# Score matmul of the small key halves over 128 rows instead of 64, and a new order of the next pair's projections

## The chip, the cores and the metric

The kernel runs on one core of a Trainium2 chip. The metric is the device time of one execution in microseconds (us). The core has a matrix engine (PE, with its weight loads shown as PEld), a vector engine (DVE), a scalar engine (ACT), a GpSimd engine (POOL), and a queue engine (SP) that issues nearly all DMA transfers here. Each engine works through its own instructions in order.

## The reference

A decoder trunk of two layers over 1024 tokens of 1024 features, in f32. Each layer has twelve mixer heads of 64 features and four memory heads, one output projection, and a gated feed-forward block with a short convolution. Layer 0 mixes with a forgetting bias, layer 1 with rotary embedding and a fixed table of dilated windows.

```python
sc = einsum('bhqd,bhkd->bhqk', qi, k) * scale      # layer 0
sc = sc + ci[..., :, None] - c[..., None, :]
sc = where(kpos <= qpos, sc, NEG); p = softmax(sc)
out = einsum('bhqk,bhkd->bhqd', p, v)
...
h = h + merge_heads(concat([mix, mem_out])) @ w_out
h = h + conv_ffn(rmsnorm(h, norm_ffn), w_up, conv_w, conv_b, w_down)
```

## The kernel before, in words

Every f32 operand is split into a large half (hi) and a small rest (lo), and a product is made of three PE passes: hi·hi, hi·lo, lo·hi (`mm3g`, L162 to L164). Activations stand transposed, features on the 128 partitions; tokens are cut into two halves of 512.

The attention phase of a layer handles the twelve mixer heads as six pairs. A pair's queries and keys are projected by `proj_q` and `proj_k`, each in two halves of 512 tokens; a half takes 24 matmuls of 512 columns. For each head, the 128 rows of a query tile (qa, qb) hold the head's 64 features of hi and the 64 of lo. The key tile (ka, kb) holds the keys' hi twice, the second copy made by a DMA from SP (`move`, L95), so that one matmul over 128 rows gives (q hi + q lo)·(k hi). The keys' lo of both heads share one tile kl, 64 rows each.

A step is one tile of 128 queries of one head: eight steps i = 0..7 make a head, sixteen a pair, 96 a layer. `scores` (called from `emit_s`) makes the scores of step i against (i+1)*128 keys, in pieces of at most 512 columns: L376 over 128 rows, L377 over 64 rows (q hi · k lo), and in layer 0 for the last piece of a step a mask matmul in bf16 (L379). A layer has 144 pieces (over both layers: 48 each of 128, 256 and 384 columns, and 144 of 512). DVE then adds the bias and takes the extreme (L380), ACT the exponential (L384), DVE the reciprocal and the scaling (L386, L387). Two steps later PE transposes the result (L393) and ACT and DVE split it (L394, L395); one more step later, for two steps at a time, PE multiplies with the values (L692), and `fold` sends the rows to memory.

What PE does between these is other work, dealt out by `Fill`: a list of generators (projections of the next pair, values of the next two pairs by `proj_v`, at the end the output projection `out_part`), each with a cost, a deadline and an earliest step. At each step `Fill.at` sets a rate from the costs and deadlines, and `Fill.go` issues groups of three matmuls by it. PE's order is that in which the code is written; for the other engines a scheduler sets it. Key and query tiles come from a pool of ten (`qk`).

`out_part` reads the other pairs' attention output back through SP (`oraw`, L253); ACT and POOL split it (L254, L255).

Of the kernel before, what the change touches and what calls it, by code (L numbers as in the profile page):

```python
# [29 lines left out]
def trunk(ctx, tc, a, out):  # L30
# [90 lines left out]
    def norm_stages(acc, psum, n=4):  # L121
        """acc [P, n*128]: sums of squares per partition -> PSUM [P, n*128], rstd on each partition."""
        st = psum()
        for t in range(n):
            nc.tensor.matmul(st[:, t:t + 1], lhsT=acc[:, t * P:(t + 1) * P], rhs=ones[:, 0:1], start=True, stop=True)
        ms = small("nms")
        nc.vector.tensor_scalar(ms[:, :n], st[:, :n], 1.0 / T, EPS, op0=ALU.mult, op1=ALU.add)
        rs = small("nrs")
        nc.gpsimd.tensor_tensor(rs[:, :n], ms[:, :n], mhalf[:, :n], op=ALU.pow)
        dg = sqt("dg").rearrange("p (n q) -> p n q", n=4)  # L130
        nc.vector.tensor_tensor(dg[:, :n, :], ident.unsqueeze(1).to_broadcast([P, n, P]),  # L131
                                rs[:, :n].unsqueeze(2).to_broadcast([P, n, P]), op=ALU.mult)
        yield None
        rb = psum()
        nc.tensor.matmul(rb[:, :n * P], lhsT=ones, rhs=dg[:, :n, :], start=True, stop=True)  # L135
        yield rb
# [10 lines left out]
    def norm_split(h_k, rb, gi, hi, lo):  # L147
        """hi/lo of h * rstd * gain for each feature tile."""
        for k in range(KD):
            w = h_k(k).shape[-1]  # L150
            xn = sqt("xn")
            nc.vector.scalar_tensor_tensor(xn[:, :w], h_k(k), gains[:, gi, k:k + 1], rb[:, :w],
                                           op0=ALU.mult, op1=ALU.mult)
            nc.scalar.copy(hi(k), xn[:, :w])
            eng = nc.gpsimd if k % 2 else nc.vector
            eng.tensor_tensor(lo(k), xn[:, :w], hi(k).bitcast(F32), op=ALU.subtract)

# [1 line left out]
    def mm3g(ps, whi, wlo, xhi, xlo, nk, cost=0, first=True, last=True):  # L159
        """ps = sum_k w_k^T x_k; yields after each k."""  # L160
        for k in range(nk):
            nc.tensor.matmul(ps, lhsT=whi(k), rhs=xhi(k), start=(first and k == 0), stop=False)  # L162
            nc.tensor.matmul(ps, lhsT=whi(k), rhs=xlo(k), start=False, stop=False)  # L163
            nc.tensor.matmul(ps, lhsT=wlo(k), rhs=xhi(k), start=False, stop=(last and k == nk - 1))  # L164
            yield 3 * cost
# [11 lines left out]
    def put_v(dst, ps):  # L177
        """dst [P, 2, 128] <- even head [hi | lo], odd head [lo | hi]."""
        s = ps.rearrange("p (h d) -> p h d", h=2)
        f = dst.rearrange("p h (s d) -> p (h s) d", s=2)  # L180
        dh = f[:, 0::3, :]
        nc.scalar.copy(dh, s)
        nc.vector.tensor_tensor(f[:, 1:3, :], s, dh.bitcast(F32), op=ALU.subtract)

# [48 lines left out]
    def h_tiles(half):  # L233
        """residual stream, one half of the tokens, transposed: f(n) -> [P, HT]."""
# [11 lines left out]
    def load_o(l, half):  # L246
        """hi/lo of rows of O^T, but for the last pair's."""
# [29 lines left out]
    # ================= attention phase =================  # L277
    def attention_phase(l):
        with tc.manual_schedule(engines={mybir.EngineType.PE}):
# [6 lines left out]
            vts = {}  # L286

            def proj_v(g):
                """values of two pairs: a generator for each half of the tokens."""
# [29 lines left out]
            def proj_fm(hl, half, rope):  # L319
                """128 projected features (two heads) x 512 tokens, in f32."""  # L320
# [15 lines left out]
            def proj_q(wi, half, dst, rope):  # L336
                """queries of two heads: a stack of (hi, lo) for each."""
# [10 lines left out]
            def proj_k(wi, half, dst, rope):  # L348
                """keys of two heads: hi twice for each, lo of both in one."""
                if half == 0:  # L350
                    dst["w" + str(wi)] = load_w(a[f"wq{l}"][wi])
                    dst["k"], dst["kl"] = (qk("ka"), qk("kb")), qk("kl")
                src, eng = yield from proj_fm(dst["w" + str(wi)], half, rope)
                hs = slice(half * HT, half * HT + HT)
                for i, t in enumerate(dst["k"]):
# [3 lines left out]
                    eng.tensor_tensor(dst["kl"][r, hs], src[r, :], t[r, hs].bitcast(F32), op=ALU.subtract)  # L359
# [3 lines left out]
            def proj_qk(p, half):  # L363
                yield from proj_q(2 + 2 * p, half, ops[p], l == 1)
                yield from proj_k(3 + 2 * p, half, ops[p], l == 1)

# [1 line left out]
            def scores(y, m, qst, q2, kst, k2, i, nk, bias, tri):  # L368
                qs = slice(i * P, (i + 1) * P)
                npc = (nk + HT - 1) // HT  # L370
                for pc in range(npc):
# [5 lines left out]
                    nc.tensor.matmul(sw, lhsT=q2[:, qs], rhs=k2[:, c0:c1], start=False, stop=not mask)  # L377
# [19 lines left out]
            def fold(o, odd, c, half):  # L397
                """sum of the products with V's hi and lo halves -> rows of O^T in DRAM."""
# [96 lines left out]
            def forget():  # L495
                """c = cumsum(log_sigmoid(z)) over tokens; -8c goes to c_scr as rows."""
# [29 lines left out]
            class Fill:  # L526
                """pieces of other products, spread over the steps so that each is done by its deadline."""
# [68 lines left out]
            kms = [k.rearrange("p (x h t) -> p x h t", x=2, h=2) for k in (vk[:, T:], qk("km"))]  # L596
# [23 lines left out]
            QK, V, OP = 48 * 216, 96 * 113, 168 * 216  # L620
            v0 = proj_v(0)
            if l == 0:
# [4 lines left out]
                fill.add(proj_qk(0, 0), QK, 0)  # L627
                fill.add(f, 0, 0)
                fill.add(proj_qk(0, 1), QK, 0)
            else:  # L630
                fill.add(proj_qk(0, 0), QK, 0)
                fill.add(proj_qk(0, 1), QK, 0)
# [6 lines left out]
            for p in range(1, NPAIR):  # L639
                g = p // 2  # L640
                v = proj_v(g) if p % 2 == 0 else None
                fill.add(proj_qk(p, 0), QK, 16 * p - (1.5, 2.5)[l], 16 * p - 16, ("a", p))
                fill.add(proj_qk(p, 1), QK, 16 * p + (2.5, 1.5)[l], 16 * p - 16, ("b", p))
                if v:
                    fill.add(v[0], V, 16 * p + 2, 16 * p - 13, ("va", p))
# [7 lines left out]
            def emit_s(s):  # L653
# [12 lines left out]
                rows = slice(64 * hh, 64 * hh + 64)  # L666
                scores(y, m, qst[hh], qst[hh][rows, :], kst[hh], kl[rows, :], i, (i + 1) * P, bias, l == 0)
# [62 lines left out]
    # ================= output projection and FFN =================  # L730
    def ffn_phase(l):
# [130 lines left out]
def _layouts(i):  # L862
# [5 lines left out]
    def fm(w, n):  # L868
        """[.., 1024, n*128] -> [n, 128, 8*128]: for each block of columns, rows on partitions."""
        return w.reshape(KD, P, n, P).transpose(2, 1, 0, 3).reshape(n, P, KD * P)  # L870

    def nat(w):
        """[1024, n] -> [2, 128, 4*n]"""
# [39 lines left out]
    # constants that depend on shapes alone  # L913
# [35 lines left out]
```

## Time and profile before

| | |
|---|---|
| time, median of 3 runs | 2742.74 us (2741.11 to 2742.86) |
| span of the profiled execution | 2742.4 us |
| PE busy | 2633.8 us (96%) |
| DVE busy | 1467.9 us (54%) |
| ACT busy | 1113.3 us (41%) |
| POOL busy | 894.9 us (33%) |

The profiled execution is given by its span; it lies 0.3 us under the median, so nothing of size lies outside the span. Busy is the share of time in which an engine has an instruction under way. Matmuls overlap, so a busy PE can still lose time inside: what counts there is the distance from one matmul's start to the next one's. PEclk is the granted clock: 1.00 is 2.4 GHz, 0.50 is 1.2 GHz.

### The profile page before, as it was taken

What the parts mean: (1) busy time and instruction counts of PE and PEld (TensorE: products, weight loads), DVE (VectorE), ACT (ScalarE), POOL (GpSimd) and SP (SyncE); (2) the same over time, 40 slices, a digit from 0 to 9 for tenths busy, and PEclk for the clock granted to TensorE, in tenths of its full rate; (3) what the DMA queues carried; (4) which work ended last, traced back from release to release, by engine and by line L of the source; (5) the groups of instructions that cost most, each with busy time, mean ns of one, the idle gap of its engine ahead of it and who ended that gap; (6) DMA issues with size and microseconds to landing.
All of it is one profiled execution on the core that took longest, in us unless ns stands there. A gap on an engine that the chain in (4) does not pass through costs nothing. (4 is left out here: it accounts for less than half of the span.)

```text
span 2742.4 us, 34430 instructions
## 1 busy us (share of the span) xinstructions
PE 2633.8 (96%) x12808; PEld 2129.9 (78%) x12808; DVE 1467.9 (54%) x2879; ACT 1113.3 (41%) x2149; POOL 894.9 (33%) x650
## 2 busy tenths in 40 slices
PE   5999999899999999999998999998899999999997
PEld 4877878667888888888777777776678888888886
DVE  6667666556434342434766766665654343434345
ACT  4555454444313131323355666664443122222222
POOL 4201010345323232323452333335543232322332
PEclk8999999999999999999998999999999999999999
DMA  5122112322111111111331111123111111111112
GB/s 166 47 70 61 46 57 70 121 88 66 50 54 47 47 51 50 47 48 59 127 117 37 42 34 39 39 85 124 64 61 46 54 47 46 51 50 47 47 53 93
DMA packets 95055, 174.65 MB, mean 64 GB/s; under 512 B 11932, under 2 KB 14620, under 8 KB 94888
## 3 DMA queue, kind: packets, MB, share of 16 engines
q1 hardware_dynamic: 94024, 171.77, 19.5%
q8 instruction: 101, 1.65, 0.2%
q10 hardware_dynamic: 864, 0.69, 0.1%
q14 instruction: 66, 0.54, 0.1%
HBM read 148.24 MB, written 15.78 MB: 60 GB/s over the span
## 5 line engine op out<-in xcount | busy, mean ns | idle before, releaser
L110 POOL TENSOR_TENSOR wlo<-wraw,whi 128x512 fp32r<-128x512 f32 x450 | 590.2, 1332 | 1483.8 <-ACT whi L109 1335.0
L162 PE MATMUL bk<-xh,whi 128*128 128x512 f32 x2112 | 863.1, 409 | 32.8 <-ACT xh L254 11.9
L163 PE MATMUL bk<-xl,whi 128*128 128x512 f32 x2112 | 832.4, 394 | 4.2 <-POOL xl L255 2.5
L164 PE MATMUL bk<-xh,wlo 128*128 128x512 f32 x2112 | 830.7, 393 | 0.5 <-POOL wlo L110 0.5
L109 ACT CAST whi<-wraw 128x512 fp32r<-128x512 f32 x450 | 268.2, 616 | 684.4 <-PE bk L163 459.2
L162 PEld LDWEIGHTS bk<-xh,whi 128*128 128x128 f32 x2112 | 402.7, 191 | 125.0 <-ACT xh L254 13.1
L164 PEld LDWEIGHTS bk<-xh,wlo 128*128 128x128 f32 x2112 | 401.0, 190 | 86.4 <-POOL wlo L110 1.2
L163 PEld LDWEIGHTS bk<-xl,whi 128*128 128x128 f32 x2112 | 401.9, 190 | 81.5 <-POOL xl L255 6.2
L162 PE MATMUL bk<-gh,whi 128*128 128x512 f32 x704 | 275.4, 391 | 1.2 <-DVE h L259 1.1
L767 DVE SCALAR_TENSOR_TENSOR gate<-bk,cw,gate 128x511 f32<-128x511 f32 (+1 forms) x176 | 131.2, 746 | 271.3 <-ACT gate L765 269.7
L163 PE MATMUL bk<-gl,whi 128*128 128x512 f32 x704 | 274.1, 389 | 0.0
L164 PE MATMUL bk<-gh,wlo 128*128 128x512 f32 x704 | 273.8, 389 | 0.0
L259 DVE TENSOR_TENSOR h<-h,bk 128x512 f32<-128x512 f32 x208 | 141.6, 685 | 233.8 <-PE bk L164 233.8
L384 ACT ACTIVATE y<-y,m 128x128 f32<-128x128 f32 (+1 forms) x192 | 149.2, 777 | 118.8 <-DVE m L380 116.2
L767 DVE SCALAR_TENSOR_TENSOR val<-bk,cw,val 128x511 f32<-128x511 f32 (+1 forms) x176 | 131.1, 745 | 115.2 <-ACT val L765 113.6
L395 DVE TENSOR_TENSOR ptl<-bk,pth 128x512 fp32r<-128x512 f32 (+3 forms) x288 | 152.8, 552 | 73.6 <-ACT pth L394 71.3
L394 ACT CAST pth<-bk 128x512 fp32r<-128x512 f32 (+3 forms) x288 | 130.5, 479 | 101.7 <-PE bk L393 99.3
L162 PEld LDWEIGHTS bk<-gh,whi 128*128 128x128 f32 x704 | 132.2, 188 | 31.1 <-DVE h L259 2.7
L163 PEld LDWEIGHTS bk<-gl,whi 128*128 128x128 f32 x704 | 132.2, 188 | 27.6 <-issue 0.5
L164 PEld LDWEIGHTS bk<-gh,wlo 128*128 128x128 f32 x704 | 132.2, 188 | 27.5
L783 DVE TENSOR_TENSOR gl<-val,gh 128x1024 fp32r<-128x1024 f32 x44 | 53.9, 1226 | 174.8 <-ACT gh L782 174.8
L779 POOL TENSOR_TENSOR val<-val,gate 128x1024 f32<-128x1024 f32 x44 | 105.8, 2404 | 90.1 <-ACT gate L778 90.1
(160 smaller groups left out, 3662.3 us busy)
## 6 DMA issues: line engine op xcount, KB each, us to landing
wraw<-in_wu SPq DMA_DIRECT2D x176, 256.0 KB, 2.8
wraw<-in_wd SPq DMA_DIRECT2D x104, 256.0 KB, 2.8
wraw<-in_wo SPq DMA_DIRECT2D x64, 256.0 KB, 2.8
wraw<-in_wq SPq DMA_DIRECT2D x56, 256.0 KB, 2.8
oscr<-fold SPq DMA_DIRECT2D x56, 128.0 KB, 2.2
oraw<-oscr SPq DMA_DIRECT2D x28, 256.0 KB, 3.9
cb<-cscr SPq DMA_DIRECT2D x12, 512.0 KB, 3.8
wraw<-in_wv SPq DMA_DIRECT2D x20, 256.0 KB, 2.8
```

What stands on the lines that cost most here:

```text
L109: nc.scalar.copy(hi[:, w], raw[:, :n])
L110: nc.gpsimd.tensor_tensor(lo[:, w], raw[:, :n], hi[:, w].bitcast(F32), op=ALU.subtract)
L162: nc.tensor.matmul(ps, lhsT=whi(k), rhs=xhi(k), start=(first and k == 0), stop=False)
L163: nc.tensor.matmul(ps, lhsT=whi(k), rhs=xlo(k), start=False, stop=False)
L164: nc.tensor.matmul(ps, lhsT=wlo(k), rhs=xhi(k), start=False, stop=(last and k == nk - 1))
L259: nc.vector.tensor_tensor(H[half](n), (src or H[half])(n), ps, op=ALU.add)
L384: nc.scalar.activation(y[:, :nk], y[:, :nk], AF.Exp, bias=m[:, npc - 1:npc], scale=-1.0, accum_out=m[:, 2:3])
L394: nc.scalar.copy(ph, tp[:, :nj, :])
L395: nc.vector.tensor_tensor(pl, tp[:, :nj, :], ph.bitcast(F32), op=ALU.subtract)
L767: nc.vector.scalar_tensor_tensor(t[:, o + d:o + HT], ps[:, :HT - d], w(2 - d), t[:, o + d:o + HT], op0=ALU.mult, op1=ALU.add)
L779: nc.gpsimd.tensor_tensor(v, v, g, op=ALU.mult)
L783: nc.vector.tensor_tensor(gl, v, gh.bitcast(F32), op=ALU.subtract)
```

## The change

The lo halves of the keys get a tile for each head (kla, klb), with the lo rows in both halves of the partitions; the second copy is made by a DMA on SP, as for hi. The second score matmul reads the same 128-row query tile as the first and contracts over 128 rows; it adds q lo · k lo. Queries and keys of the next pair become separate entries of the fill list: queries in the first head of the current pair, then the first half of the values, then keys in the second head. A pair now takes six tiles of the pool of ten instead of five; the memory keys' tile km moves to another pool.

```diff
-                    dst["k"], dst["kl"] = (qk("ka"), qk("kb")), qk("kl")
+                    dst["k"], dst["kl"] = (qk("ka"), qk("kb")), (qk("kla"), qk("klb"))
...
                     nc.scalar.copy(t[r, hs], src[r, :])
                     move(t[o, hs], t[r, hs])
-                    eng.tensor_tensor(dst["kl"][r, hs], src[r, :], t[r, hs].bitcast(F32), op=ALU.subtract)
+                    eng.tensor_tensor(u[r, hs], src[r, :], t[r, hs].bitcast(F32), op=ALU.subtract)
+                    move(u[o, hs], u[r, hs])
...
                     nc.tensor.matmul(sw, lhsT=qst[:, qs], rhs=kst[:, c0:c1], start=True, stop=False)
-                    nc.tensor.matmul(sw, lhsT=q2[:, qs], rhs=k2[:, c0:c1], start=False, stop=not mask)
+                    nc.tensor.matmul(sw, lhsT=qst[:, qs], rhs=klt[:, c0:c1], start=False, stop=not mask)
...
-            kms = [k.rearrange("p (x h t) -> p x h t", x=2, h=2) for k in (vk[:, T:], qk("km"))]
+            km = yt("km").bitcast(R32)
+            kms = [k.rearrange("p (x h t) -> p x h t", x=2, h=2) for k in (vk[:, T:], km)]
...
-            QK, V, OP = 48 * 216, 96 * 113, 168 * 216
+            QK, V, OP = 24 * 216, 96 * 113, 168 * 216
...
-                fill.add(proj_qk(p, 0), QK, 16 * p - (1.5, 2.5)[l], 16 * p - 16, ("a", p))
-                fill.add(proj_qk(p, 1), QK, 16 * p + (2.5, 1.5)[l], 16 * p - 16, ("b", p))
+                fill.add(pair_q(p, 0), QK, 16 * p - 12, 16 * p - 16, ("a", p))
+                fill.add(pair_q(p, 1), QK, 16 * p - 8, 16 * p - 16, ("a", p))
                 if v:
-                    fill.add(v[0], V, 16 * p + 2, 16 * p - 13, ("va", p))
+                    fill.add(v[0], V, 16 * p - 6, 16 * p - 13, ("va", p))
+                fill.add(pair_k(p, 0), QK, 16 * p - (1.5, 2.5)[l], 16 * p - 8, ("a", p))
+                fill.add(pair_k(p, 1), QK, 16 * p + (2.5, 1.5)[l], 16 * p - 8, ("b", p))
+                if v:
                     fill.add(v[1], V, 16 * p + 6, 16 * p - 13, ("vb", p))
```

The lines of the changed file stand three further down here (L376, L377, L379 and L393 become L379, L380, L382 and L396).

PE in layer 0, pair 2, second head, between the scores of steps 45 and 46. Before, with one group of three projection matmuls on either side of the transposes:

```order
L162 MATMUL bk<-xh_567,whi 128x512
L163 MATMUL bk<-xl_568,whi 128x512
L164 MATMUL bk<-xh_567,wlo 128x512
L393 MATMUL bk<-ident,y 128x128 x4
L162 MATMUL bk<-xh_567,whi 128x512
L163 MATMUL bk<-xl_568,whi 128x512
L164 MATMUL bk<-xh_567,wlo 128x512
L376 MATMUL bk<-kb,qb 128x512
```

Of the change, the same place, ahead of it the scores of step 45:

```order
L379 MATMUL bk<-kb,qb 128x512
L380 MATMUL bk<-klb,qb 128x512
L379 MATMUL bk<-kb,qb 128x256
L380 MATMUL bk<-klb,qb 128x256
L382 LDWEIGHTS identb
L382 MATMUL bk<-trim,identb 128x128
L396 MATMUL bk<-ident,y 128x128 x4
L162 MATMUL bk<-xh_567,whi 128x512
L163 MATMUL bk<-xl_568,whi 128x512
L164 MATMUL bk<-xh_567,wlo 128x512
```

One group of three has left this step. Over whole heads the projection work, counted in matmuls of 512 columns, goes in layer 0 from 42, 42 to 48, 36 in the two heads of pair 0, from 66, 80 to 86, 71 in those of pair 1, and from 74, 63 to 96, 36 in those of pair 2; in layer 1 the second heads of pairs 0, 2 and 4 go from 66 to 42 each.

SP in layer 1 near the end of the fifth pair, where the last pair's keys and the read-back for the output projection (oraw) follow each other. Before:

```order
L253 DMA oraw<-oscr_0_87 128x512
L95 DMA ka<-ka 64x512
L95 DMA kb<-kb 64x512
L409 DMA oscr_4_91<-fold 64x512
L253 DMA oraw<-oscr_1_88 128x512
L253 DMA oraw<-oscr_2_89 128x512
```

Of the change:

```order
L253 DMA oraw<-oscr_0_87 128x512
L95 DMA ka<-ka 64x512
L95 DMA kla<-kla 64x512
L95 DMA kb<-kb 64x512
L95 DMA klb<-klb 64x512
L412 DMA oscr_4_91<-fold 64x512
L253 DMA oraw<-oscr_1_88 128x512
L253 DMA oraw<-oscr_2_89 128x512
```

Two copies of lo rows stand between the first and the second read-back.

## Rows read from the trace of the kernel before

**Rows 1.** Windows, attention steps of both layers: length, busy by engine, PEclk, DMA, GB/s.

```profile
168.50:493.20 324.70, 324.27 (x1884) 253.41 (x1883) 225.70 (x602) 170.80 (x393) 34.50 (x27) 1.00 0.20 60
1499.00:1840.40 341.40, 337.11 (x1904) 264.65 (x1903) 233.98 (x609) 219.18 (x478) 111.18 (x85) 1.00 0.16 45
```

**Rows 2.** Timeline of PE, layer 1: start, duration, line, operands.

```profile
1547.19 0.40 PE L376 MATMUL bk<-kb,qb 128*128 128x512 f32 x1
1547.51 0.50 PE L377 MATMUL bk<-kl,qb 64*128 64x512 f32 x1
1547.94 0.39 PE L376 MATMUL bk<-kb,qb 128*128 128x256 f32 x1
...
1548.57 0.50 PE L162 MATMUL bk<-xh,whi 128*128 128x512 f32 x1
1548.91 0.39 PE L163 MATMUL bk<-xl,whi 128*128 128x512 f32 x1
1549.14 0.39 PE L164 MATMUL bk<-xh,wlo 128*128 128x512 f32 x1
1549.37 0.60 PE L393 MATMUL bk<-ident,y 128*128 128x128 f32 x4
...
1550.04 0.39 PE L163 MATMUL bk<-xl,whi 128*128 128x512 f32 x1
```

**Rows 3.** Timeline of PE, layer 0: value products, then masked scores.

```profile
334.80 0.29 PE L692 MATMUL bk<-ptl,vt 128*128 128x256 f32 x1
334.92 0.22 PE L692 MATMUL bk<-pth,vt 128*128 128x128 f32 x1
334.98 0.28 PE L692 MATMUL bk<-ptl,vt 128*128 128x128 f32 x1
...
338.43 0.39 PE L376 MATMUL bk<-kb,qb 128*128 128x512 f32 x1
...
339.68 0.23 PE L379 MATMUL bk<-trim,identb 128*128 128x128 bf16 x1
...
340.03 0.40 PE L163 MATMUL bk<-xl,whi 128*128 128x512 f32 x1
```

**Rows 4.** Timeline of PE's weight loads, layer 0.

```profile
330.86 0.19 PEld L376 LDWEIGHTS bk<-kb,qb 128*128 128x128 f32 x1
331.36 0.18 PEld L377 LDWEIGHTS bk<-kl,qb 64*128 64x128 f32 x1 [0.31 <-issue]
```

**Rows 5.** All waits: PEld at L377, total us and times.

```profile
PEld bk L377 <- issue: 63.1, 228, 0.4
```

**Rows 6.** Windows of three heads, columns as in rows 1.

```profile
168.50:190.80 22.30, 22.30 (x108) 15.39 (x107) 18.32 (x51) 12.58 (x30) 2.55 (x2) 1.00 0.17 47
323.40:355.60 32.20, 32.20 (x172) 24.20 (x171) 22.79 (x60) 16.71 (x37) 1.31 (x1) 1.00 0.15 41
1667.60:1700.50 32.90, 32.90 (x167) 24.58 (x166) 22.30 (x56) 23.04 (x48) 10.76 (x9) 1.00 0.12 33
```

**Rows 7.** Groups of DVE instructions in one head: a query half's subtractions.

```profile
L346 DVE TENSOR_TENSOR qa<-bk,qa 64x512 fp32r<-64x512 f32 x2 | 1.4, 684 | 1.2 <-ACT qa L345 1.1
```

**Rows 8.** Waits of PE: total us, times, longest.

```profile
PE bk L162 <- ACT xh L254: 11.9, 3, 5.8
PE bk L376 <- DMA ka<-ka: 2.3, 2, 1.1
```

**Rows 9.** Timeline of POOL, layer 1: the key's lo rows of one head.

```profile
1548.11 1.28 POOL L359 TENSOR_TENSOR kl<-ropeq,ka 64x512 fp32r<-64x512 f32 x1 [1.46 <-ACT ka L357]
```

**Rows 10.** DMA issues: count, KB each, median us to landing.

```profile
ka<-ka SPq DMA_DIRECT2D x24, 128.0 KB, 2.2
```

**Rows 11.** Window where layer 0's last pair begins, columns as in rows 1.

```profile
493.20:520.00 26.80, 19.81 (x97) 14.16 (x95) 12.76 (x32) 14.08 (x30) 12.57 (x10) 0.87 0.58 183
```

**Rows 12.** Timeline of PE in that window, after its longest wait.

```profile
513.10 0.63 PE L164 MATMUL bk<-xh,wlo 128*128 128x512 f32 x1
513.52 0.63 PE L162 MATMUL bk<-xh,whi 128*128 128x512 f32 x1
```

More of the change, by code (lines that the diff above doesn't have):

```diff
@@ L351, in proj_k @@
                     dst["w" + str(wi)] = load_w(a[f"wq{l}"][wi])
-                    dst["k"], dst["kl"] = (qk("ka"), qk("kb")), qk("kl")
+                    dst["k"], dst["kl"] = (qk("ka"), qk("kb")), (qk("kla"), qk("klb"))
                 src, eng = yield from proj_fm(dst["w" + str(wi)], half, rope)
                 hs = slice(half * HT, half * HT + HT)
-                for i, t in enumerate(dst["k"]):
+                for i, (t, u) in enumerate(zip(dst["k"], dst["kl"])):
                     r, o = slice(64 * i, 64 * i + 64), slice(64 - 64 * i, 128 - 64 * i)
@@ L358, in proj_k, with pair_q, pair_k, scores @@
                     move(t[o, hs], t[r, hs])
-                    eng.tensor_tensor(dst["kl"][r, hs], src[r, :], t[r, hs].bitcast(F32), op=ALU.subtract)
+                    eng.tensor_tensor(u[r, hs], src[r, :], t[r, hs].bitcast(F32), op=ALU.subtract)
+                    move(u[o, hs], u[r, hs])
             ops = {p: {} for p in range(NPAIR)}
[L363 to L368, printed above, removed]
+            def pair_q(p, half):
+                return proj_q(2 + 2 * p, half, ops[p], l == 1)
+            def pair_k(p, half):
+                return proj_k(3 + 2 * p, half, ops[p], l == 1)
+            def scores(y, m, qst, kst, klt, i, nk, bias, tri):
                 qs = slice(i * P, (i + 1) * P)
@@ L626, in attention_phase @@
                 fill.add(f, 0, 0)
-                fill.add(proj_qk(0, 0), QK, 0)
+                fill.add(pair_q(0, 0), QK, 0)
+                fill.add(pair_k(0, 0), QK, 0)
                 fill.add(f, 0, 0)
-                fill.add(proj_qk(0, 1), QK, 0)
-            else:
-                fill.add(proj_qk(0, 0), QK, 0)
-                fill.add(proj_qk(0, 1), QK, 0)
+                fill.add(pair_q(0, 1), QK, 0)
+                fill.add(pair_k(0, 1), QK, 0)
+            else:
+                for half in range(2):
+                    fill.add(pair_q(0, half), QK, 0)
+                    fill.add(pair_k(0, half), QK, 0)
                 fill.add(v0[0], V, 0)
@@ L665, in emit_s @@
                 y, m = yt("y"), new_m()
-                rows = slice(64 * hh, 64 * hh + 64)
-                scores(y, m, qst[hh], qst[hh][rows, :], kst[hh], kl[rows, :], i, (i + 1) * P, bias, l == 0)
+                scores(y, m, qst[hh], kst[hh], kl[hh], i, (i + 1) * P, bias, l == 0)
                 st["y", s] = y
```

## The prediction

> **What bounds the kernel now.** I read the windows over the attention steps first. In layer 0 PE is busy for 324.3 of 324.7 us, in layer 1 for 337.1 of 341.4, at a clock of 1.00; DVE comes next with 70% and 69%, ACT with 53% and 64% [rows 1]. So in these 666 us time is what PE's instructions take from start to start. Nothing outside the attention phases is changed, and they are the only place to look.
>
> Then PE's timeline, for those distances. Between ordinary full matmuls of 512 columns it is 0.23 us (L163 to L164) [rows 2]; for 256 columns it is 0.12, for 128 columns 0.06 [rows 3]. The score matmuls don't keep this. In layer 1 a step with a piece of 512 and one of 256 columns runs from 1547.19 (first L376) to 1548.91 (L163, the second projection matmul behind it): 1.72 us [rows 2]. Its matmuls at the ordinary distances would take three times 0.23 (two halves of the 512 piece, and L162) and two times 0.12, 0.93 in all. The excess is 0.79 us for two 64-row matmuls, **0.395 us each**. In layer 0, 512 and 128 columns with a mask run from 338.43 to 340.03 [rows 3], 1.60 us against 0.69 + 0.12 = 0.81: again 0.79, with the mask's matmul inside it. Small and large pieces lose the same, so it isn't the columns; it is the passage to 64 rows and back. The weight loads show the first half of it: L376's load begins at 330.86, L377's only at 331.36, after an idle 0.31 [rows 4], and such an idle stands before 228 of the 288 loads of L377, 63 us in all [rows 5].
>
> **The change part by part.**
>
> *The second matmul over 128 rows.* Its columns stay, so it costs an ordinary distance, and the excess goes. 288 pieces, 144 per layer, 96 of them with a mask (the last piece of each of layer 0's 96 steps). The 192 without: 192 x 0.395 = **75.8 us**. With a mask, the mask matmul had its time hidden in the passage and will need its own. No row shows a bf16 matmul behind a full f32 one. From below it costs 0.06, as any 128 columns [rows 3]; from above, if its change of type cost what the change of rows does, the whole 0.395. I take the nearest row: four transposes of 128 columns, which also differ in kind from their neighbours, take with one projection matmul 1550.04 - 1549.37 = 0.67 us [rows 2], less 0.23, so 0.11 each. That leaves 0.285 x 96 = **27.4 us** (0 to 32.2).
>
> *The new order of the projections.* PE's total of projection work is the same. But second heads of pairs 0, 2 and 4 now hold 36 (layer 0) or 42 (layer 1) projection matmuls, and there DVE, which has the same scores to treat, comes close to PE. Layer 0, the head at 323.40: 32.2 us for 63 projection matmuls [rows 6]; with 36, 27 x 0.23 = 6.2 less, twelve pieces x 0.395 = 4.7 less, eight masks x 0.11 = 0.9 more: PE 22.2 us. DVE had 22.8; 27 projection matmuls are 27/24 of a half, and each half has two subtractions of 0.684 [rows 7], so 1.5 less: 21.3, or 96% of PE's time. Layer 1, the head at 1667.60: 32.9 - 24 x 0.23 - 4.7 = 22.7 for PE; DVE 22.3 - 1.4 = 20.9, 92%. The first head of layer 0 goes from 42 to 48: 22.3 + 1.4 - 4.7 + 0.9 = 19.9, DVE about 18.7, 94%. The highest share of DVE at which PE lost nothing is that head's 18.3/22.3 = 82% [rows 6]; 100% is out of reach with its waits for ACT. I take 88%: the heads then last 24.1 instead of 22.2 (three of them), 23.8 instead of 22.7 (three), 21.3 instead of 19.9: 5.7 + 3.3 + 1.4 = **10 us lost** (0 at 100%, 22 at 82%). The other heads get more projection work, and DVE is no neighbour there.
>
> *The copies of the keys' lo rows.* 48 more DMAs of 128 KB on SP, which land in 2.2 us like ka's [rows 10]. Before, PE waited for that copy twice, 1.1 us each, in layer 1 [rows 8]. The copy of kla can start only after POOL's subtraction, 1.28 us later than ka's [rows 9]. First halves of the keys now end in the fourth step before their use where the next pair is odd, and second halves earlier than before. So some 1.3 us more at three places in layer 1, less the two old waits: **2 us lost** (0 to 8). In layer 0 the subtraction is on DVE and there is no rotation ahead of it; nothing.
>
> *The same copies in front of the read-back.* SP issues in order, and where the last pair begins, the read-back of the attention output stands behind the last key copies. There PE already waits, 11.9 us over both layers, 5.8 the longest [rows 8]; the window has PE busy for 19.8 of 26.8 us and a clock of 0.87 [rows 11], and behind the wait the distance of two full matmuls is 0.42 us, the lower level of 1.2 GHz [rows 12]. kla and klb stand in this queue now and make the loads wait for DVE (layer 0) or two POOL subtractions (layer 1): 1.4 and 2.6 us. And PE arrives earlier by what it saved in the three steps before (3 to 5 pieces, some 1.5 us, and fewer projection matmuls), which turns into wait. **8 us lost** over both layers (3 to 15, the latter if the lower clock lasts longer).
>
> *At nothing:* the pool of ten tiles (six for a pair, two for the next queries; the four key tiles come when the first head has given three back), and km's move. The cover is the second head, 22 us long; without it keys would wait for the last score of the pair.
>
> Sum: 75.8 + 27.4 - 10 - 2 - 8 = 83 us. From the profiled 2742.4, 2659.2; the median lies 0.3 higher: **2659.5 us**.
>
> **The rivals.**
>
> *The loads stay exposed.* The weights of two neighbouring full matmuls use the same rows of the array. If a load could not run under a matmul of the same rows, two loads of 0.19 [rows 4] would remain of each 0.395, 288 x 0.015 = 4 us would be won, the losses above would be hidden under it, and the time would be about 2742. Against it stands the distance of 0.23 at L163 to L164 [rows 2]: a load of 0.19 doesn't fit beside 512 columns unless it overlaps. The Trainium skill ("TensorE: Matmul & The Clock Gate", Part 3, What overlaps and what doesn't) says that loads overlap with matmuls in flight only when the row group differs; the trace disagrees for full matmuls, and shows the opposite at the change of row group. 2 in 100.
>
> *DVE takes over.* If the masks give nothing back (75.8 alone) and the light heads run at a DVE share of 82%: 75.8 - 22 - 2 - 8 = 44, so 2699. For it: 92 to 96% is more than any stretch before has shown. Against: DVE's work can be put off within a head, since scores run two steps ahead. 10 in 100.
>
> *Slower, by late keys.* The lo copy misses its step at each of the ten pair changes, PE waits, and the clock falls behind the wait as it does in rows 12. A clock of 0.87 over 26.8 us [rows 11] is 7 us at half speed, 3.5 lost. With a wait of 8 us: 10 x 11.5 = 115, so 2742.4 - 83 + 115 = 2774. It decides from 8.9 us per pair change on, which is a wait of 5.4. For it: a wait for ka existed. Against: it was 1.1 us, and only in layer 1. 4 in 100.
>
> **How the numbers follow.** The forecast's case, with losses between their bounds, holds 81 in 100; a larger gain than 105 us 3. With all masks at 0.06 and the least losses (3) the time is 75.8 + 32.2 - 3 = 105 lower, 2637; with the masks at nothing and losses of 22, 8 and 15 it is 31 lower, 2711. The range is 2638 to 2697: it leaves out the upper rivals and the tails. A measurement of this kernel can tell about 0.2% (5.5 us) from no change. Faster by more than that: 0.94; within it: 0.02; slower: 0.04.
>
> **What would show it.** L377's successor (L380) without idle before its weight load, and 0.23 between it and its neighbours at 512 columns; the distance behind the mask shows its price. The light heads, 22 to 24 us long, with DVE at 85 to 92% and PE waiting for DVE's or ACT's tiles there. Waits for kla in layer 1 of 1 to 3 us in all, and the wait at L254 longer than 12. Wrong would be: an idle that stays before the second load; a mask that costs 0.3; or waits of several us at pair changes with the clock down.

## The result, and the profile after

The changed kernel takes 2701.49 us (median of 4 runs, 2698.09 to 2704.73); beside it the kernel before took 2742.80. The ratio is 0.985 (95% interval 0.9836 to 0.9864): some 41 us faster, half of the 83 that were forecast, and above the forecast's range. The profiled executions differ by 2742.4 - 2698.3 = 44.1 us. Of the kernels e1_even and e9_best below, one execution each (4225.05 and 3239.57 us) ran for long at the lower clock and is left out.

In the changed kernel the second score matmul stands on L380 and the mask's on L382; DVE's reduction is L383, the scaling L390, the transposes L396, ACT's and DVE's halves of the split L397 and L398, the value products L701. Heads are counted 0 to 11 in each layer; heads 10 and 11 are the last pair.

Windows of the profile after: the first ten heads of layer 0 and of layer 1, then head 5 of layer 0, head 5 of layer 1, and head 10 of layer 0. Columns as in [rows 1].

```profile
166.30:472.00 305.70, 293.51 (x1891) 253.86 (x1890) 223.69 (x603) 171.73 (x394) 35.83 (x28) 0.99 0.25 72
1471.90:1803.30 331.40, 304.24 (x1910) 265.86 (x1909) 225.41 (x610) 220.89 (x480) 112.88 (x87) 0.99 0.18 49
317.60:343.00 25.40, 22.52 (x145) 19.19 (x144) 21.67 (x59) 16.39 (x37) 2.58 (x2) 1.00 0.27 74
1639.90:1668.10 28.20, 23.89 (x144) 19.98 (x142) 21.82 (x58) 21.16 (x45) 10.22 (x8) 1.00 0.14 38
472.00:516.90 44.90, 39.10 (x202) 30.87 (x201) 24.97 (x65) 24.18 (x50) 19.54 (x15) 0.92 0.50 156
```

Against [rows 1], the ten heads fell from 324.7 to 305.7 us and from 341.4 to 331.4. PE's busy time fell by 30.8 and 32.9 us, but PE, which had 0.4 and 4.3 us without work, now has 12.2 and 27.2. Second heads of an even pair, which [rows 6] shows at 32.2 and 32.9 us, last 25.4 and 28.2, where 24.1 and 23.8 were forecast. DVE's share there is 85% and 77%, below the 88% at which the forecast set its limit, and PE waits all the same.

Timeline of PE after, layer 1, a step with two pieces of 512 columns; columns as in [rows 2].

```profile
1528.48 0.40 PE L379 MATMUL bk<-kb,qb 128*128 128x512 f32 x1
1528.72 0.39 PE L380 MATMUL bk<-klb,qb 128*128 128x512 f32 x1
...
1529.41 0.39 PE L162 MATMUL bk<-xh,whi 128*128 128x512 f32 x1
1529.63 0.40 PE L163 MATMUL bk<-xl,whi 128*128 128x512 f32 x1
```

From the first L379 to L163 it takes 1.15 us: five times 0.23, and no excess is left.

Timeline of PE after, layer 0, a masked step with 512 and 128 columns.

```profile
459.56 0.40 PE L379 MATMUL bk<-kb,qb 128*128 128x512 f32 x1
459.80 0.39 PE L380 MATMUL bk<-klb,qb 128*128 128x512 f32 x1
460.02 0.22 PE L379 MATMUL bk<-kb,qb 128*128 128x128 f32 x1
460.08 0.28 PE L380 MATMUL bk<-klb,qb 128*128 128x128 f32 x1
460.20 0.23 PE L382 MATMUL bk<-trim,identb 128*128 128x128 bf16 x1
460.24 0.48 PE L162 MATMUL bk<-xh,whi 128*128 128x512 f32 x1
460.56 0.40 PE L163 MATMUL bk<-xl,whi 128*128 128x512 f32 x1
```

The like step of before took 1.60 us ([rows 3]); this takes 1.00, which is 0.19 above the ordinary distances. The mask's own distance is only 0.04, but the matmul ahead of it goes on for 0.12 where 128 columns take 0.06, and L162 behind it for 0.32 instead of 0.23. Over all masked steps with a projection matmul behind, the medians by shape lie 0.12 to 0.18 above the ordinary distances, most at 0.13; the mask's own columns are in that.

PE's waits after, first ten heads of layer 1: total us, times, longest.

```profile
PE bk L396 <- DVE ptl L398: 18.7, 16, 2.7
PE bk L701 <- DVE ptl L398: 5.2, 10, 1.0
...
PE bk L380 <- DMA kla<-kla: 0.3, 1, 0.3
```

With two small ones left out here (2.7 us) these are 26.9 of the 27.2 us. In the ten heads of layer 0 the first of them comes to 9.9 us in 12 waits, of 11.9 in all. So PE's transposes now stop for a bank which DVE's L398 has not yet read, 28 times; before, this wait came 2 times in the whole program (3.1 us) and not in these windows. The key copies that the prediction feared cost 0.3 us.

What such a wait looks like, in head 9 of layer 0 (444.9 to 472.0). PE:

```profile
447.25 0.95 PE L396 MATMUL bk<-ident,y 128*128 128x128 f32 x7
...
448.97 0.23 PE L382 MATMUL bk<-trim,identb 128*128 128x128 bf16 x1
451.02 1.32 PE L396 MATMUL bk<-ident,y 128*128 128x128 f32 x8 [1.82 <-DVE ptl L398]
...
452.57 0.63 PE L163 MATMUL bk<-xl,whi 128*128 128x512 f32 x1
453.00 0.63 PE L164 MATMUL bk<-xh,wlo 128*128 128x512 f32 x1
```

ACT in the same stretch:

```profile
447.45 0.62 ACT L109 CAST whi<-wraw 128x512 fp32r<-128x512 f32 x1
448.51 0.58 ACT L345 CAST qb<-bk 64x512 fp32r<-64x512 f32 x1 [0.44 <-DVE qa L346]
449.11 0.97 ACT L397 CAST pth<-bk 128x512 fp32r<-128x512 f32 x2
```

DVE:

```profile
447.79 0.69 DVE L346 TENSOR_TENSOR qa<-bk,qa 64x512 fp32r<-64x512 f32 x1
448.50 1.01 DVE L390 TENSOR_SCALAR y<-y,m 128x128 f32<-128x128 f32 x1
449.55 0.69 DVE L346 TENSOR_TENSOR qb<-bk,qb 64x512 fp32r<-64x512 f32 x1
450.27 1.16 DVE L398 TENSOR_TENSOR ptl<-bk,pth 128x512 fp32r<-128x512 f32 x2
```

Seven transposes fill both of the transposes' banks by 448.20. ACT could split them from then on, but a query half that was just projected stands ahead in its queue: qb's cast waits 0.44 us for DVE's subtraction of qa from the same bank, then runs, and L397 starts at 449.11. DVE likewise does qb's subtraction first and comes to L398 at 450.27. PE's next transposes start at 451.02. The Trainium skill ("Perfetto Trace Analysis", Tensor Engine Instruction) says that PE may pull a weight load ahead, while ACT, DVE and GpSimd take their instructions strictly in order. The trace agrees: ACT idles until 448.51 in front of qb, with L397's input ready since 448.20.

In layer 1, head 2, the queue is longer, since a half is also rotated (L330 to L333). PE, ACT, DVE and POOL:

```profile
1559.60 0.71 PE L396 MATMUL bk<-ident,y 128*128 128x128 f32 x5
...
1563.65 0.28 PE L164 MATMUL bk<-whi,xl 128*128 128x256 f32 x1
1566.63 0.55 PE L396 MATMUL bk<-ident,y 128*128 128x128 f32 x3 [2.70 <-DVE ptl L398]
```

```profile
1563.37 0.62 ACT L345 CAST qa<-ropeq 64x512 fp32r<-64x512 f32 x1 [1.51 <-DVE ropeq L333]
1564.02 0.61 ACT L345 CAST qb<-ropeq 64x512 fp32r<-64x512 f32 x1
1564.66 0.58 ACT L405 COPY fold<-bk 64x512 f32<-64x512 f32 x1
1565.27 0.59 ACT L397 CAST pth<-bk 128x512 fp32r<-128x512 f32 x1
```

```profile
1561.57 1.77 DVE L333 TENSOR_TENSOR ropeq<-ropeq,ropeqs 128x512 f32<-128x512 f32 x1 [0.67 <-POOL ropeqs L332]
...
1565.88 0.89 DVE L398 TENSOR_TENSOR ptl<-bk,pth 128x512 fp32r<-128x512 f32 x2
```

```profile
1560.26 1.28 POOL L332 TENSOR_TENSOR ropeqs<-ropeqs,ropes 128x512 f32<-128x512 f32 x1 [1.02 <-ACT ropeqs L330]
1561.50 1.29 POOL L110 TENSOR_TENSOR wlo<-wraw,whi 128x512 fp32r<-128x512 f32 x1
```

The transposes have been ready since 1560.31, but ACT sits idle for 1.51 us in front of qa's cast, for a rotation that goes from ACT to POOL to DVE, and takes qb and a fold before L397 at 1565.27, five us later. The rotation's last link, L333, took 1.77 us where its shortest takes 0.69; up to 1.1 of the 2.70 us are that (see the last section).

**Work and excess of a head.** To set these waits beside the gain, each matmul of a head is given its ordinary distance (0.23 us for 512 columns, 0.17 for 384, 0.12 for 256, 0.06 for 128, 0.11 for a transpose), a 64-row matmul 0.39 more, a mask none, so that the price of a mask stands in the excess. What a head lasts beyond that is its excess. In us, for all heads but the last of each layer (which has other work behind it):

| head | before: length, work | after: length, work | excess before, after |
|---|---|---|---|
| layer 0, head 3 | 36.8, 35.8 | 31.0, 28.9 | 1.0, 2.1 |
| layer 0, head 9 | 31.4, 30.9 | 27.1, 20.7 | 0.5, 6.3 |
| layer 1, head 2 | 35.4, 33.0 | 37.4, 31.0 | 2.4, 6.4 |
| layer 1, head 5 | 32.9, 32.3 | 28.1, 22.1 | 0.6, 6.0 |
| heads 10 of both layers | 102.9, 78.4 | 94.4, 66.3 | 24.5, 28.1 |
| 22 heads | 769.0, 728.5 | 731.6, 625.5 | 40.5, 106.1 |

The work fell by 103.0 us. The excess rose by 65.6, so the heads won 37.4.

### The profile page after: what moved, and what is told of

Its sections match the earlier page's. It is cut to its first block, busy times and chain, and to the rows that moved or that the text cites. A ratio compares the mean times of both kernels' runs of the same rounds, so it can differ in the third digit from the quotient of the medians.

```text
span 2698.3 us, 34564 instructions
## 1 busy us (share of the span) xinstructions
PE 2549.5 (94%) x12808; PEld 2125.7 (79%) x12808; DVE 1449.2 (54%) x2879; ACT 1113.6 (41%) x2149; POOL 889.8 (33%) x650
## 5 line engine op out<-in xcount | busy, mean ns | idle before, releaser
L110 POOL TENSOR_TENSOR wlo<-wraw,whi 128x512 fp32r<-128x512 f32 x450 | 590.2, 1331 | 1422.3 <-ACT whi L109 1328.3
L162 PE MATMUL bk<-xh,whi 128*128 128x512 f32 x2112 | 857.4, 406 | 34.6 <-ACT xh L254 11.6
L163 PE MATMUL bk<-xl,whi 128*128 128x512 f32 x2112 | 832.4, 394 | 5.8 <-POOL xl L255 3.1
L162 PEld LDWEIGHTS bk<-xh,whi 128*128 128x128 f32 x2112 | 402.5, 191 | 116.9 <-ACT xh L254 13.6
L163 PEld LDWEIGHTS bk<-xl,whi 128*128 128x128 f32 x2112 | 402.2, 190 | 83.2 <-POOL xl L255 6.4
L162 PE MATMUL bk<-gh,whi 128*128 128x512 f32 x704 | 276.1, 392 | 1.2 <-DVE h L259 1.1
L163 PE MATMUL bk<-gl,whi 128*128 128x512 f32 x704 | 274.6, 390 | 0.0
L398 DVE TENSOR_TENSOR ptl<-bk,pth 128x512 fp32r<-128x512 f32 (+3 forms) x288 | 152.8, 551 | 66.1 <-ACT pth L397 65.4
L397 ACT CAST pth<-bk 128x512 fp32r<-128x512 f32 (+3 forms) x288 | 131.0, 479 | 93.1 <-PE bk L396 90.8
L396 PE MATMUL bk<-ident,y 128*128 128x128 f32 x864 | 130.2, 277 | 33.1 <-DVE ptl L398 32.9
L162 PEld LDWEIGHTS bk<-gh,whi 128*128 128x128 f32 x704 | 132.6, 188 | 31.2 <-DVE h L259 2.8
L163 PEld LDWEIGHTS bk<-gl,whi 128*128 128x128 f32 x704 | 132.6, 188 | 27.7 <-issue 0.5
L164 PEld LDWEIGHTS bk<-gh,wlo 128*128 128x128 f32 x704 | 132.4, 188 | 27.6
```

Source lines behind the costliest of these rows:

```text
L110: nc.gpsimd.tensor_tensor(lo[:, w], raw[:, :n], hi[:, w].bitcast(F32), op=ALU.subtract)
L396: nc.tensor.transpose(tp[:, jj, :], y[:, j * P:(j + 1) * P], ident)
L397: nc.scalar.copy(ph, tp[:, :nj, :])
L398: nc.vector.tensor_tensor(pl, tp[:, :nj, :], ph.bitcast(F32), op=ALU.subtract)
```

## The experiments

The theories, once the result was known. **A**: the new spread leaves the second heads of even pairs so little projection work that ACT and DVE, with their own work, bound them. **B**: with the faster scores, the chain of one step (reduction, exponential, scaling, transposes, split) bounds every head. **C**: the copies of the keys, or the pool of ten tiles. **D**: the taking out of a projected half stands in ACT's and DVE's queues ahead of the draining of the transposes' banks; at the old pace PE came to the next transposes late enough not to notice.

Twelve kernels ran, in three groups of four on one chip each; e3 to e6 and e12 ran once. Executions of the changed kernel itself differ by 6.6 us. "Ten heads" are the first ten of a layer, as in the windows above.

### e1_even and e12_even_look: the spread evened out

```diff
-                fill.add(pair_q(p, 0), QK, 16 * p - 12, 16 * p - 16, ("a", p))
-                fill.add(pair_q(p, 1), QK, 16 * p - 8, 16 * p - 16, ("a", p))
+                fill.add(pair_q(p, 0), QK, 16 * p - 8, 16 * p - 16, ("a", p))
                 if v:
                     fill.add(v[0], V, 16 * p - 6, 16 * p - 13, ("va", p))
+                fill.add(pair_q(p, 1), QK, 16 * p - 5, 16 * p - 16, ("a", p))
```

> The change with another spread: the second half of the next pair's queries is projected in the second head, so that the light heads hold 57 to 66 projection matmuls again instead of 36 or 42. Theory A (the gain went where a head holds so little projection work that the DVE and ACT chain of the scores is longer than PE's work): the light heads lose their excess of 5 to 7 us, 2665 to 2685 us. Theory B (at PE's new pace the chain limits every head, however the work is spread): no difference, 2693 to 2705. Theory C (the copies of the lo rows or the pool of ten tiles hold PE): no difference either.

Measured: 2707.51 us, ratio 0.9869 (0.9853 to 0.9886): no better than the change. The profile of the same kernel is that of e12_even_look.

> The kernel of e1, whose profile was taken at half the clock throughout and can't be read. Theory D: the light heads, with 21 to 30 more projection matmuls than in the change, lose less than there, but heads that were calm in the change lose more, each about 1 to 3 us per half taken out; the sum of the lengths of the heads is that of the change within 10 us.

Measured: 2709.7 us, span 2707.9. Ten heads of layer 0 take 296.2 us (305.7 with the change), of layer 1 346.2 (331.4). In layer 1 the wait of the transposes for L398 grows:

```profile
PE bk L396 <- DVE ptl L398: 26.3, 15, 3.8
```

In layer 0 the evened spread is worth 9.5 us, so far A holds. In layer 1 it loses 14.8: this wait grows by 7.6 (18.7 with the change), those for the copies of the keys from 0.3 to 5.3, and the clock goes to 0.97. The excess there grows in the light heads (heads 1, 5 and 9: 18.9 to 27.8 us) as well as in the others. As the cause of the whole loss A falls; and of theory D's expectation the sum of the heads holds (642.4 against 637.1 us), but not that the light heads lose less in layer 1.

### e2_order_only: the kernel before with the new order alone

```diff
-                fill.add(proj_qk(p, 0), QK, 16 * p - (1.5, 2.5)[l], 16 * p - 16, ("a", p))
-                fill.add(proj_qk(p, 1), QK, 16 * p + (2.5, 1.5)[l], 16 * p - 16, ("b", p))
+                fill.add(proj_q(2 + 2 * p, 0, ops[p], l == 1), QK // 2, 16 * p - 12, 16 * p - 16, ("a", p))
...
+                fill.add(proj_k(3 + 2 * p, 0, ops[p], l == 1), QK // 2, 16 * p - (1.5, 2.5)[l], 16 * p - 8, ("a", p))
```

> The kernel before with the new spread of projections alone, 64-row matmuls and one lo tile kept, no new copies. Theory A: PE's work in the light heads is 4.7 us longer than in the change, so it stays above DVE's, and the spread costs little: 2743 to 2755 us. If the spread costs as much at any pace: 2770 to 2785. Theory C: 2741 to 2745.

Measured: 2751.97 us, ratio 1.0036 (1.0023 to 1.0049): the order alone costs 9 us. The windows of the ten heads (324.7 and 341.4 us before), and a wait of PE in the whole program:

```profile
166.30:497.40 331.10, 326.83 (x1891) 254.85 (x1889) 227.61 (x605) 171.81 (x394) 35.76 (x28) 1.00 0.20 60
1500.00:1850.60 350.60, 343.16 (x1910) 267.47 (x1909) 227.39 (x613) 220.80 (x481) 113.02 (x87) 0.99 0.15 42
```

```profile
PE bk L393 <- DVE ptl L395: 12.7, 12, 1.6
```

So the waits come with the order in part, at the old pace too; full rows bring the rest (30 waits, 32.9 us, with the change in the whole program). Of the 15.6 us that the ten heads are longer, 2.7 are work moved here from the heads 10; the order's excess is 12.9, all of it in the light heads (the first head of layer 0 and the second heads of even pairs: 14.3). With the same order and full rows it is 51.6 (without the masks' price), 22.9 of them in other heads: that difference comes with the pace (the new copies' own waits are 0.3 us). From here to the changed kernel it is 2752.0 - 2701.5 = 50.5 us.

### e3_no_scale: less work for DVE

```diff
-                nc.vector.reciprocal(m[:, 3:4], m[:, 2:3])
-                nc.vector.tensor_scalar(y[:, :nk], y[:, :nk], m[:, 3:4], None, op0=ALU.mult)
```

> The change without the reciprocal and the scaling of the exponentials (the softmax denominator is left out), which takes some 0.7 us of DVE work and one DVE link of the chain out of each step. Theories A and B: the light heads, 25 to 29 us long now, shrink to 21 to 23, and the time to 2650 to 2670 us. Theory C: heads stay as long as they are, 2695 to 2705.

Measured: 2690.98 us; ten heads 295.8 and 329.2. The window of layer 1:

```profile
1462.90:1792.10 329.20, 302.77 (x1910) 264.73 (x1909) 179.05 (x455) 219.12 (x480) 113.61 (x87) 0.99 0.18 50
```

DVE has 46 us less to do in these ten heads, and one link of the step's chain is gone; they win 2.2 us, and the transposes' wait for the split is still 29.3 us in the whole program. In layer 0 it helps more (9.9 us). Neither DVE's amount of work nor B explains layer 1. The time lies between the two ranges that were expected.

### e4_tp3: three banks for the transposes, two for the scores

```diff
-    NB = {"s": 3, "p": 2, "tp": 2, "o": 1}
+    NB = {"s": 2, "p": 2, "tp": 3, "o": 1}
```

The feed-forward phase's lists of banks are changed with it.

> The change with three PSUM banks for the transposes and two for the scores instead of two and three. If the waits of the transposes for DVE's ptl are a want of banks: they go, and the time falls by 10 to 20 us, 2680 to 2690. If DVE is late as a whole (A and B): the wait only moves to another instruction, 2693 to 2710.

Measured: 2688.39 us; ten heads 299.9 and 329.1. PE's waits in the whole program:

```profile
PE bk L396 <- DVE ptl L398: 13.8, 12, 2.3
PE bk L701 <- DVE ptl L398: 12.1, 14, 1.4
```

With one bank more PE can run further ahead of the split, and 19.1 us of the transposes' waits go; but the value products then wait more for the same L398 (7.8 us with the change), and the scores for their banks, of which there are fewer (7.7 us). The same engines are late; part of the wait shifts. The time lies in the range for a want of banks, but of the 11.7 us between the spans 5.0 lie behind the heads 10 (the heads 11, the feed-forward phases and what stands between them), and layer 1's ten heads win only 2.3.

### e5_no_evac: projected halves are made, but not taken out

All pairs then use the queries and keys of pair 0. The keys' function is changed as that of the queries:

```diff
+                if keep is not None:
+                    dst["q"] = keep["q"]
...
+                    yield from mm3g(psp(), cols(hi), cols(lo), lambda k: xh[:, k, :], lambda k: xl[:, k, :], KD, 216)
+                    return
...
-                return proj_q(2 + 2 * p, half, ops[p], l == 1)
+                return proj_q(2 + 2 * p, half, ops[p], l == 1, ops[0] if p else None)
```

> The change, with the projections of pairs 1 to 5 made but their results not taken out of PSUM: all pairs use pair 0's queries and keys (that part of the computation is left out). Theory D (PE's transposes wait because the draining of their banks stands behind the taking out of a projection half on ACT and DVE, which wait there for each other and in layer 1 for POOL): though this takes only some 3 us of DVE work out of a head against 6 without the scaling, which gave 9 us, it frees more, 2655 to 2670 us, and layer 1's heads give most. Theory B (the scores' own chain is the limit at PE's new pace): 2685 to 2698.

Measured: 2651.07 us, span 2649.3. Windows of the ten heads of both layers, and of head 2 of layer 1:

```profile
164.40:460.00 295.60, 290.38 (x1892) 252.59 (x1890) 199.21 (x565) 150.24 (x356) 36.15 (x28) 1.00 0.18 56
1457.80:1757.20 299.40, 294.39 (x1911) 262.77 (x1909) 201.43 (x573) 152.41 (x366) 38.87 (x30) 1.00 0.13 40
1513.00:1544.50 31.50, 31.50 (x208) 28.55 (x207) 21.20 (x60) 16.63 (x40) 5.08 (x4) 1.00 0.15 43
```

PE's work and its order are the same as with the change. The 22 heads take 683.8 us instead of 731.6: 47.8 of the 65.6 us come back, 32.0 of them in layer 1's ten heads; 11.4 of the rest is the masks' price. Head 2 goes from 37.4 to 31.5, with PE never idle. C isn't tested apart here (the copies go too, and the tiles of the pool of ten are no longer renewed), but the copies' waits were 0.3 us, and e6 and e7 leave both in place.

### e6_no_rope: no rotation in layer 1

```diff
-                return proj_q(2 + 2 * p, half, ops[p], l == 1)
+                return proj_q(2 + 2 * p, half, ops[p], False)
```

and the same for the keys.

> The change without the rotation of queries and keys in layer 1 (left out), so that a half is taken out there as in layer 0. Theory D: layer 1's excess, 59 us in its eleven heads against 43 in layer 0, falls to layer 0's, 2680 to 2690 us. Theory B: layer 1's chain of the scores is unchanged, 2693 to 2700.

Measured: 2658.66 us, span 2656.9: more than was expected. The ten heads of layer 1, and its head 5:

```profile
1460.90:1764.70 303.80, 295.09 (x1911) 263.14 (x1909) 224.31 (x613) 173.62 (x404) 38.27 (x30) 1.00 0.21 57
1615.80:1640.60 24.80, 23.32 (x143) 20.03 (x142) 21.63 (x59) 16.00 (x37) 2.60 (x2) 1.00 0.20 53
```

Layer 0 stays at 305.7 us. In layer 1 27.6 us come back there, though DVE has only 1.1 us less to do (it makes lo in POOL's place). So DVE's busy time isn't what PE pays for: head 5 runs at a DVE share of 87% and takes 24.8 us, where it took 28.2 at 77%. ACT has 47.3 us less to do and POOL 74.6, so this run alone doesn't divide the rotation's chain from its load on ACT; the timeline above shows ACT idle at the chain's end, and e8 bears on it below. Of the 41.4 us between the spans, 11.1 lie between the start of head 11 of layer 0 and the first head of layer 1, where the first pair's halves are rotated.

### e7_pool_evac and e8_pool_evac_tp3: POOL takes the halves out

In layer 0 ACT copies the bank once and POOL makes hi and lo from the copy; in layer 1 POOL also does the rotation's last addition and the hi casts. e8 adds the banks of e4.

```diff
+                if not rope and pool:
+                    q = sqt("pq")
+                    nc.scalar.copy(q, ps)
+                    return q, nc.gpsimd
...
-                nc.vector.tensor_tensor(q, q, qs, op=ALU.add)
+                nc.gpsimd.tensor_tensor(q, q, qs, op=ALU.add)
...
-                    nc.scalar.copy(t[r, hs], src[r, :])
+                    (nc.gpsimd.tensor_copy if pool else nc.scalar.copy)(t[r, hs], src[r, :])
```

> The change with the taking out of pairs' projection halves moved: in layer 0 ACT copies the whole bank once and POOL makes hi and lo, in layer 1 POOL also makes the last addition of the rotation and the hi part. ACT and DVE then wait for nothing in it. Theory D: 2660 to 2680 us. Theory B: 2690 to 2700. A rival to D: POOL's four operations of 1.3 us in a row make keys late, or slow DVE down, 2700 to 2720.

> The run before, with three PSUM banks for the transposes and two for the scores. If both act on the same wait, little is added to the better of the two: 2660 to 2680 us. If they act on different waits (theory B for the banks): 2645 to 2665.

Measured: e7 2671.99 us, ratio 0.9743 (0.9728 to 0.9758); e8 2663.68, ratio 0.9713 (0.9697 to 0.9729). Windows of e8, ten heads of each layer and head 5 of layer 1, and its wait in the whole program:

```profile
165.40:459.50 294.10, 290.68 (x1891) 251.97 (x1890) 201.96 (x563) 159.66 (x373) 113.65 (x109) 1.00 0.26 75
1453.30:1763.80 310.50, 299.34 (x1910) 263.17 (x1908) 216.98 (x591) 197.76 (x441) 163.37 (x144) 1.00 0.19 52
1611.30:1636.40 25.10, 23.82 (x143) 20.01 (x143) 20.55 (x56) 18.43 (x40) 14.88 (x14) 1.00 0.13 36
```

```profile
PE bk L400 <- DVE ptl L402: 8.2, 11, 1.8
```

The work is all done, only elsewhere, and 30 and 38 us come back; the transposes' wait falls from 32.9 to 18.3 in e7 and 8.2 in e8. Of e8's 36.6 us between the spans, 11.6 and 20.9 lie in the ten heads of the two layers (8.7 and 18.4 in e7) and 9.1 between the attention phases. Head 5 of layer 1 takes 25.1 us with ACT at 73% and DVE at 82%, where it took 28.2 at 75% and 77%: neither engine was full there. The two heads 10 lose: 94.4 us with the change, 99.4 in e7, 101.3 in e8. What e8 adds to e7 lies in both of the ranges that were expected of it, so it doesn't tell whether both act on one wait.

### e9_best: the last pair taken out as before

```diff
-                return proj_q(2 + 2 * p, half, ops[p], l == 1, True)
+                return proj_q(2 + 2 * p, half, ops[p], l == 1, p < NPAIR - 1)
```

and the same for the keys; in the last pair the rotation's addition goes back to DVE.

> Run e8 with the last pair's halves taken out by ACT and DVE as in the change, since in e7 and e8 the two last-pair stretches are 5 to 7 us longer than in the change (99.4 and 101.3 us against 94.4): its keys, late from POOL, stand in SP's queue before the read-back. If that is the reason: 94 to 96 us there and 2655 to 2660 us in all. If not: 2662 to 2666.

Measured: 2664.95 us, ratio 0.9712 (0.9696 to 0.9728), no different from e8. That POOL's part in the last pair costs time isn't borne out. The length of e9's own heads 10 isn't known; in e10, which takes the last pair out in the same way, they last 95.7 us.

### e10_best_even: e9 with the spread of e1

The edit is e1's.

> e9 with the spread of e1, 57 to 66 projection matmuls in the light heads. Theory A, which e1 spoke against, could still hold once the taking out no longer blocks: then 2640 to 2650 us. Theory D alone: no difference to e9, within 6 us.

Measured: 2693.62 us, ratio 0.9819 (0.9804 to 0.9834): 29 us slower than e9. PE's longest wait in the ten heads of layer 1, and the window of its head 6:

```profile
PE bk L384 <- DMA kla<-kla: 8.2, 6, 1.7
```

```profile
1655.30:1696.10 40.80, 35.19 (x204) 31.97 (x205) 22.43 (x64) 20.24 (x45) 16.73 (x15) 0.83 0.18 46
```

With the second half of the queries in the second head the keys come later, and PE waits for the copies (8.2 for kla and 3.2 for ka; 1.5 us in all in e8); the clock is 0.83 in a head that took 33.8 us in e8. Against e8 the ten heads lose 12.7 and 23.3 us. How this divides among its causes isn't settled. Here the uneven spread of the change is the better one, against A; the expectation from D alone, no difference, failed too, since the late copies (C) cost time here.

### e11_before_best: the kernel before with POOL's taking out and three banks

The edits are those of e9, on the kernel before.

> The kernel before with POOL taking out the halves of all pairs but the last and three banks for the transposes: 64-row matmuls, one lo tile, the spread of before. Theory D says that PE's slower scores hid the blocking, so freeing it is worth little there: 2730 to 2744 us. If the blocking cost the kernel before as much: 2700 to 2715.

Measured: 2739.04 us (2728.97 to 2740.00), ratio 0.9972 (0.9956 to 0.9988). What is worth 37 us on the changed kernel is worth 4 by the medians on the old one (3 to 12 by the interval; two of the six executions took 2729), and in the profile its ten heads are no shorter (326.6 and 342.9 us). The range of D is met. But the old kernel has the old order too, with 3.1 us of this wait in all, so the run doesn't tell whether the slow scores or the old order kept the wait away; that the pace counts is shown by e2 against the change, which have the same order.

## Why the prediction was wrong

The sign was right and the size was not; it failed at the step on the new order of the projections: 10 us at the light heads and nothing at the others.

- **The 64-row excess (75.8 us, and the 0.395 behind the masks): right.** Unmasked steps show an excess of 0.00 to 0.11 (medians by shape, with a projection matmul behind; the 0.09 to 0.11 stand where the last piece has 128 columns or a piece of 512 and one of 256 make the step, some 0.3 us in a head). In the 22 heads the work falls by 264 x 0.39 = 103.0 us. That loads stay exposed, the first rival, is refuted by the distances of 0.23 at L380.
- **The masks at 0.11: nearly right.** About 0.13, which is 96 x 0.02 = 2 us more.
- **The late copies of the keys (2 us) and the read-back (8 us): too high.** 0.3 us in the ten heads of layer 1, where the two old waits, 2.3 us together, went. The wait at L254 is 11.6 us in all, no longer than before. The two heads 10 have 3.6 us more excess, 1.0 of it masks (8 x 0.13).
- **The light heads at 10 us: a third of the size, and in layer 1 the wrong cause.** The seven heads that the prediction listed gained 32.9 us of excess, 28.7 without the masks of four of them (32 x 0.13 = 4.2). The prediction sized them by a DVE share that can't exceed some 88%. In layer 1 its 3.3 us became 16.6, at shares of 73 to 77%; there DVE was not full, as e6 and e8 show, and taking work from it (e3) gives back 0.3. In layer 0 its 7.1 us became 12.1, at 81 to 85%; there e3 gives back 6.6 and e5 7.5, so that the runs don't tell a DVE that is nearly full from one that is held up. A share says nothing of the order in which an engine takes its work.
- **"The other heads get more projection work, and DVE is no neighbour there": wrong.** They gained 29.1 us, 22.9 without masks (48 x 0.13 = 6.2). Layer 1's head 2, with DVE at 26.0 of 37.4 us, even became longer than before.

The last two steps make 28.7 + 22.9 = 51.6 us where 10 stood: 41.6 too few. At the old pace the new order alone costs 12.9 (e2). With 2 too few at the masks and 7 too many at the last pair and the keys, the forecast's 83 becomes 46, and 44 were measured. The rival *DVE takes over* named 2699 us, and that it comes so near is luck: it had the masks give nothing, and they gave some 96 x 0.26 = 25 us, about what it too left out at the other heads.

Of the 51.6, PE's idle time accounts for 11.8 + 22.9 = 34.7 (the windows above against [rows 1]); the rest lies around the stops: the matmul before one runs out over 0.28 to 0.40 us instead of 0.12 to 0.23, and the clock is lower after some (0.99 over both windows, at most 6 us of 637).

What the runs showed in its place differs by layer. Of the 51.6 us, 16.1 lie in layer 0's ten heads and 35.5 in layer 1's; this is what each run gives back of them:

| run | layer 0, of 16.1 | layer 1, of 35.5 |
|---|---|---|
| e3, less work for DVE | 9.9 | 2.2 |
| e4, one bank more | 5.8 | 2.3 |
| e12, the spread evened | 9.5 | -14.8 |
| e5, halves not taken out | 10.1 | 32.0 |
| e6, no rotation in layer 1 | 0.0 | 27.6 |
| e7, POOL takes them out | 8.7 | 18.4 |
| e8, the same, one bank more | 11.6 | 20.9 |

In layer 1 it is D: the taking out of projected halves ahead of the split in ACT's and DVE's order. It is shown by taking it away (e5), by shortening its chain (e6) and by moving it to POOL with all the work still done (e7), while less work for DVE, another spread or a bank more do little or harm. That the pace brought it out is shown by e2, 12.9 us in both layers with the same order at the old pace. In layer 0 nearly every remedy gives some 10 us, so A, B and D aren't divided there; the timeline of head 9 speaks for D, and one timeline doesn't decide it. C is left with 0.3 us of waits in the change.

The prediction had a row that points to it: [rows 9] shows POOL's lo waiting 1.46 us for ACT, the same chain. It read shares, and never asked which instruction stands in front of the split when a half is done, and how early PE may come back before that shows. At the old pace the passages alone gave ACT and DVE 12 x 0.39 = 4.7 us more in each head.

Open: what divides A, B and D in layer 0, why heads 10 lengthen in e8, and how e10's loss divides. Full rows with the old order of the projections were not run; e1 is the nearest, and it changes the place of the queries' second half alone.

## What to carry to other kernels

When PE gets faster, look at each place where it will come back to a bank sooner, and read there what stands ahead of the bank's reader in the queue of each engine that empties it; in layer 1's light heads busy shares of 73 to 77% hid it. A chain over several engines, whose links wait for each other in queues in order, can cost the engines behind it the whole chain and not its busy time: give it to an engine which nobody waits for (30 us here; a bank more gave 13 alone and 8 on top). Try such a repair on the faster kernel, since on the slower one, with its own order, it showed little (4 us against 37).

## What was not expected of the hardware

- After a wait of 1.82 us PE ran at the lower level, 1.2 GHz: the distance of two matmuls of 512 columns is 0.43 us at 452.57 (above), from 452.00 until about 455.4. Half of these 3.4 us, 1.7, are lost on top of the wait; the wait of 2.70 us in layer 1 was followed by as long a stretch, from 1567.9 to 1571.3. Waits of the same length in head 5 of layer 0 (1.8) and head 6 of layer 1 (2.7) were not: both heads have a granted clock of 1.00. What makes the difference isn't shown here.
- A DVE instruction beside POOL's can take several times its time: the scaling of 128 columns took 1.01 us at 448.50 (the shortest of L390 takes 0.285) while POOL's L110 ran from 448.14 to 449.43, and L333 took 1.77 at 1561.57, while POOL's next L110 ran from 1561.50 to 1562.79 (the shortest of L333 takes 0.69). The Trainium skill, "SBUF — State Buffer", section "SBUF: two separate sides", says that a GpSimd instruction and a DVE instruction with two inputs in SBUF, or in a mode that uses both ports, share one pair of ports: the one that starts first locks it for its whole length, and the other blocks. The trace agrees, as both DVE instructions start after POOL's and end only after it does (449.51 and 1563.34, against 449.43 and 1562.79). It is a part of the waits above, at most 0.7 of the 1.82 us and 1.1 of the 2.70. It isn't their main cause: in e7 POOL has 51 to 78 us more to do in the ten heads of a layer, and they are shorter.
- The passage to 64 rows and back cost 0.395 us whatever the columns, and a bf16 mask of 128 columns between f32 matmuls, with the same rows, added some 0.13 to its step, its own columns included (0.19 in the step at 459.56, where an unmasked step of that shape already shows 0.11).
